# Where the output projection's units stand among the cached blocks of a hybrid decoder step

## The chip, the cores and the metric

The kernel runs on one core of a Trainium2 chip, in one launch. The metric is the device time of the launch in microseconds (us). TensorE (PE in the profile) multiplies, VectorE (DVE), ScalarE (ACT) and GpSimd (POOL) work elementwise and reduce, SyncE (SP) issues most transfers. Each engine runs its own instructions in the order in which the program holds them, and waits on semaphores for the others.

## The reference, cut to what matters

One decoder layer is computed for a prompt of 1024 rows (`x_prompt`, 1024 wide) and for 8 sequences of 8 new rows (`x_sample`, 64 rows), in 32 bits:

```python
n = rmsnorm(h, lw['g_mix']);  u = n @ lw['w_in']          # split for the two groups
o_gla = ...   # group A: gated linear attention, 512 wide
o_mla = attend(q_m, k_m, v_m)                             # group B: latent attention, 512 wide
h = h + jnp.concatenate([o_gla, o_mla], axis=-1) @ lw['w_o']   # the output projection
y, conv_new = conv_ffn(rmsnorm(h, lw['g_ffn']), conv_prev, lw)
h = h + y
h = h + (p @ lw['ple_w_proj']) * jax.nn.sigmoid(rmsnorm(h, lw['g_ple']) @ lw['ple_w_gate'])
```

For the prompt `attend` is a causal attention over its own rows. For each of the 8 sequences it goes over 8192 cached positions in 64 pages of 128, found by a page table: of each page, keys and values are projected from a latent of 128 numbers, the keys normed, and scores, softmax and values summed. The same `w_o` serves the prompt's rows and the sample rows.

## The kernel before, in words

**Numbers in two halves.** A 32-bit operand is split into a high and a low part (`split`, L116 on ACT for the high part, L117 on DVE or POOL for the low one), and a product is three matmuls, high by high, high by low, low by high (`mm3`, L137 to L139).

**Two streams.** The generator `cache_stream` (L646) goes over 64 blocks of 8 pages each, numbered n = 0 to 63, eight to a sequence. A block takes two steps: in the first its pages 4 to 7 are turned by transposes (`pre`: tile ctp L518, and for the rope part crp L496 and csr L506) and pages 0 to 3 go through `main` (L526); in the second the next block's pages 0 to 3 are turned and this block's pages 4 to 7 go through `main`. The first block of a sequence has the new rows as a ninth page. In `main` a page has two products `ks` of three matmuls each (320 and 256 columns), of which ACT takes the squares (tile csq, L542) and the scores (sn, L544); after every second page DVE reduces the squares (css, L547). One and two blocks later come `stage_b` (the norms, and the maximum tile ml, L568, once per block), `stage_c1` (tile mt, exponents, tile phl) and `stage_pv` (tile cpv, L612). `ks` has three PSUM banks; ctp, crp, csr, mt and cpv share two (`pm`); the dense work has three (`pd`).

The generator `dense` (from L1332) does everything else up to the feed-forward: projections, linear attention, prompt attention (`prompt_attention`, tiles S, t, o), and last `wo_prompt` (L1482). A loop written by hand (L1540 to L1554) interleaves the two: each `yield` of the dense stream gives its cost, each cache step adds 4.4 times the stage's `PACE` to the time at which the next is due, and the stream that is behind gets its turn. When the dense stream is used up, the remaining cache steps follow alone.

**The planner.** What the loop gives out is program order. A list scheduler then arranges each engine's instructions by readiness in its own model of time, with program order as the priority. `tc.keep_in_program_order(m)` pins an instruction: it can't stand ahead of the instruction given out just before it on its engine.

**The output projection before.** The mixed outputs lie transposed in DRAM (`doT`, 1024 x 1024), in eight chunks of 128 rows; chunk c is multiplied with rows c of `w_o`. `wo_chunk` (L1377) loads one chunk whole: its rows (tiles oraw, then sh and sl, 1024 columns) and its weights (tiles stg, then wdh and wdl). `down` (L1389) does one pair of chunks for all eight row tiles t and both column halves f: a unit is six matmuls of 512 columns into ps_dn and one addition to `h` on DVE (L1400). `wo_prompt` gives out pairs 0 to 2 so, 48 units in 24 yields of cost 2.6, unpinned, with two calls of `down_sample` (L1405, tile ps_ds) for the sample rows; then it loads chunks 6 and 7. The last pair's 16 units (`last_pair`, L1517, pinned) are kept as filling: `fill(k)` gives out k of them at the waits of the last block (L583 to L691: 4, 1, 3, 2 and 2), and the last four follow. Each finished row tile is normed (`normed`, L1510) for the feed-forward.

After the blocks, the attention of the sample rows is projected (po_mla, L684), `w_o`'s chunks 4 and 5 are loaded again for them, and the rows are turned for the feed-forward, whose matmuls begin near 1401 us.

Of the kernel before, what the change touches and what calls it, by code (L numbers as in the profile page):

```python
# [18 lines left out]
P = 128  # L19
D = 1024  # L20
# [25 lines left out]
def step_kernel(ctx: ExitStack, tc: tile.TileContext, A):  # L46
# [68 lines left out]
    def split(hi, lo, src, lo_eng=None):  # L115
        act.copy(hi, src)  # L116
        (lo_eng or dve).tensor_tensor(lo, src, hi.bitcast(F32), ALU.subtract)  # L117
# [18 lines left out]
    def mm3(ps, ah, al, bh, bl, first=True, last=True):  # L136
        pe.matmul(ps, ah, bh, start=first, stop=False)  # L137
        pe.matmul(ps, ah, bl, start=False, stop=False)  # L138
        pe.matmul(ps, al, bh, start=False, stop=last)  # L139
# [386 lines left out]
    def main(o, g0, cT):  # L526
        buf = o.b % 2
        if g0 == 0:
            o.sn = cp.tile([P, 9, 64], F32, tag="sn", name="sn", bufs=3)
            o.ss = cp.tile([P, 9, 8], F32, tag="css", name="css", bufs=2)  # L530
        gn = min(4, o.nt - g0)
        cTh, cTl = cT
        for i in range(gn):
            if i % 2 == 0:
                sq2 = cp.tile([P, 2, 512], F32, tag="csq", name="csq", bufs=2)
            sq = sq2[:, i % 2]
            for f in range(2):
                ks = psK.tile([P, 512], F32, tag="k", name="ks")
                w = 256 if f else 320
                mh, ml = (m[:, f * 320:f * 320 + w] for m in mv[buf])  # L540
                mm3(ks[:, :w], cTh[:, i, :], cTl[:, i, :], mh, ml)
                act.activation(sq[:, f * 256:f * 256 + 256], ks[:, 0:256], AF.Square)  # L542
                if f == 0:
                    act.copy(o.sn[:, g0 + i, :], ks[:, 256:320])  # L544
            if i % 2 or i == gn - 1:
                n = i % 2 + 1
                dve.tensor_reduce(o.ss[:, g0 + i + 1 - n:g0 + i + 1, :].rearrange("p i h -> p (i h)"),  # L547
                                  sq2[:, :n].rearrange("p i (h n) -> p (i h) n", n=64), AX.X, ALU.add)

    def stage_b(o):  # L550

# [24 lines left out]
    def stage_c1(o):  # L576

        nt = o.nt
        sb = o.sn[:, :nt, :]
        mt = pm([P, 512], "mt")  # L580
        final = (o.b, o.bi) == (NB - 1, 7)
        if final:
            fill(4)  # L583
        pe.transpose(mt[:, 0:P], o.ml.rearrange("p a c -> p (a c)"), ident)
        m = cp.tile([P, 1], F32, tag="bm", name="bm", bufs=4)
        mo = state.get(o.b)
        if mo is None:
# [10 lines left out]
        pool.tensor_tensor(phl[:, :nt, 64:128], sb, phl[:, :nt, 0:64].bitcast(F32), ALU.subtract)  # L598
# [733 lines left out]
    def dense():  # L1332
# [30 lines left out]
    chunks = {}  # L1363

    def stage(shape, dt, name):
        return z["wf"].tile(shape, dt, tag="stage", name=name, bufs=3)
# [4 lines left out]
    def fold_tile(shape, dt, name):  # L1371
        return z["wf"].tile(shape, dt, tag="fd", name=name, bufs=1)

    def wdown(rows):
        return tuple(w[:, 0] for w in wload(z["wf"], rows, 1, D, "wd", 2, 3, stg))

    def wo_chunk(c):  # L1377
        sh = z["wf"].tile([P, T], F32R, tag="sh", name="sh", bufs=3)
        sl = z["wf"].tile([P, T], F32R, tag="sl", name="sl", bufs=3)
        for c0 in range(0, T, 512):  # L1380
            raw = stage([P, 512], F32, "oraw")
            sp.dma_start(raw, doT[c * P:(c + 1) * P, c0:c0 + 512])
            split(sh[:, c0:c0 + 512], sl[:, c0:c0 + 512], raw)
        chunks[c] = (sh, sl, oTg[:, c] if c < 4 else None) + wdown(A["w_o"][0][c * P:(c + 1) * P, :])

    def hrows(t):
        return z["h"][:, t, :] if t < NT else z["hs"]

    def down(grp, bank, order, after=None):  # L1389

        h = z["h"]
        for t in order:
            tt = slice(t * P, (t + 1) * P)
            for f in range(2):
                cs = slice(f * 512, (f + 1) * 512)
                ps = bank([P, 512], "ps_dn")
                for i, c in enumerate(grp):
                    sh, sl, _, wdh, wd = chunks[c]
                    mm3(ps, sh[:, tt], sl[:, tt], wdh[:, cs], wd[:, cs], i == 0, i == len(grp) - 1)
                dve.tensor_tensor(h[:, t, cs], h[:, t, cs], ps, ALU.add)  # L1400
            if after is not None:
                after(t)
            yield 2.6

    def down_sample(parts, bank):  # L1405

        for f in range(2):
            cs = slice(f * 512, (f + 1) * 512)
            ps = bank([P, 512], "ps_ds")
            for i, (ss_, wdh, wd) in enumerate(parts):  # L1410
                pe.matmul(ps, ss_, wdh[:, cs], start=i == 0, stop=False)
                pe.matmul(ps, ss_, wd[:, cs], start=False, stop=i == len(parts) - 1)
            fold_sample(ps, f)

    def fold_sample(ps, f):
        hs = z["hs"][:, f * 512:(f + 1) * 512]
# [62 lines left out]

    room = {}  # L1480

    def wo_prompt():  # L1482

        opened("fx")
        room["hp"] = opened("hp")
        residual(z["hp"])
        room["wf"] = opened("wf", 2)
        room["fb"] = opened("fb")
        for g in range(3):
            grp = (2 * g, 2 * g + 1)  # L1490
            for c in grp:
                wo_chunk(c)
            if g == 0:
                for t in range(NT):
                    sp.dma_start(hrows(t), A["x_prompt"][0, t * P:(t + 1) * P, :])
                sp.dma_start(z["hs"], A["x_sample"].rearrange("b t d -> (b t) d"))
            yield from down(grp, pd, range(NT))
            if g < 2:
                down_sample([chunks[c][2:] for c in grp], pd)
# [14 lines left out]
        sp.dma_start(dh[t], x)  # L1514
        xnorm(t, x, pool if VIAP >> t & 1 else dve)

    def last_pair():  # L1517

        for t in order:
            tt = slice(t * P, (t + 1) * P)  # L1520
            for f in range(2):
                cs = slice(f * 512, (f + 1) * 512)
                ps = pd([P, 512], "ps_dn")
                for i, c in enumerate((6, 7)):
                    sh, sl, _, wdh, wd = chunks[c]
                    m = pe.matmul(ps, sh[:, tt], wdh[:, cs], start=i == 0, stop=False)
                    if i == 0:
                        tc.keep_in_program_order(m)
                    pe.matmul(ps, sh[:, tt], wd[:, cs], start=False, stop=False)
                    pe.matmul(ps, sl[:, tt], wdh[:, cs], start=False, stop=i == 1)  # L1530
                dve.tensor_tensor(z["h"][:, t, cs], z["h"][:, t, cs], ps, ALU.add)
                if f:
                    normed(t)
                yield
# [35 lines left out]
    def both(shape, name):  # L1570
# [1 line left out]
        return (pd, pm, pd, pm, pd, p2)[turn[0]](shape, name)  # L1572

    tw = opened("tw", side="right")
    w45 = [(z["oTm"][:, c - 4],) + tuple(w[:, 0] for w in wload(z["tw"], A["w_o"][0][c * P:(c + 1) * P, :], 1, D, "w45", 2, 3, stg))
           for c in (4, 5)]
    down_sample(w45 + [(z["oTm"][:, c - 4],) + chunks[c][3:] for c in (6, 7)], pm)
    tw.close()


# [458 lines left out]
```

## Time and profile before

| what | value |
|---|---|
| time, median of 3 runs (lowest, highest) | 2287.79 us (2287.11, 2289.05) |
| the profiled execution's own time | 2291.95 us |
| its span, first to last instruction | 2290.0 us |
| granted TensorE clock, mean | 0.981 |
| share of the span busy: PE, DVE, ACT, POOL | 95%, 72%, 58%, 54% |

The span is what the views of the trace cover; the time of an execution holds 2 us more. Times in the views are microseconds from the start of the span. A view of windows gives, for each stretch, its length, each engine's busy time with the number of instructions, the granted clock, and the share and rate of the transfers. A view of groups gives for each line, engine and tile the count, the busy time and the mean in ns of one instruction, and behind the bar the idle time ahead of them with what ended it. In a timeline a row has its start, its duration, engine, line and tiles (out<-in), and in brackets a wait ahead of it. Records of matmuls overlap, since they are pipelined; a few are missing.

### The profile page before, as it was taken

The numbers are of one execution on the slowest core, as the hardware profiler recorded it, in microseconds if no ns is written. First come the engines' busy times: TensorE is split into PE (matmuls) and PEld (weight loads), VectorE is DVE, ScalarE is ACT, GpSimd is POOL, SyncE is SP. The second block draws the span as 40 slices with busy tenths as digits, with TensorE's granted clock in tenths as the row PEclk, the third lists the DMA queues.
The fourth block names the chain that finished last, engine by engine and source line by source line (L and its number), as shares of the span: only waits on it lengthen the run. The fifth ranks groups of instructions, "written<-read, shape, count | busy, mean of one in ns | idle before, by whom it ended". The sixth has DMA issues, their size and how long they took to land.

```text
span 2290.0 us, 38701 instructions
## 1 busy us (share of the span) xinstructions
PE 2173.6 (95%) x13591; PEld 1963.1 (86%) x13591; DVE 1657.5 (72%) x2608; ACT 1335.5 (58%) x3711; POOL 1238.1 (54%) x1332
## 2 busy tenths in 40 slices
PE   7999999999999999999998876999999999999999
PEld 6889878878888888887787766999999997888899
DVE  4675776477788888887787667878888875777642
ACT  5576766777788888887657755333333334222531
POOL 5575668567777777776334547665666640010200
PEclk9899999999999999999999997999999999999999
DMA  5343344413232222214222112322223223433131
GB/s 179 103 141 102 88 128 146 130 49 95 81 94 75 62 65 68 58 45 148 89 87 63 45 74 83 102 97 93 93 92 98 88 84 120 122 118 119 49 116 40
DMA packets 193459, 213.42 MB, mean 93 GB/s; under 512 B 41198, under 2 KB 145107, under 8 KB 193267
## 3 DMA queue, kind: packets, MB, share of 16 engines
q1 hardware_dynamic: 180835, 168.47, 24.1%
q0 software_dynamic: 12432, 42.48, 6.1%
q8 instruction: 109, 1.79, 0.3%
q14 instruction: 83, 0.68, 0.1%
HBM read 168.34 MB, written 42.52 MB: 92 GB/s over the span
## 4 chain that ended last, share of the span: by engine, by line
PE 75%; DVE 8%; ACT 7%; POOL 4%; DMA 3%; issue 2%; SPq 0%; POOLq 0%; DVEq 0%; ACTq 0%
PE ps_gu L139 6%; PE ps_gu L138 6%; PE ps_gu L137 6%; PE ks L137 4%; PE ps_dn L137 4%; PE ps_dn L138 4%; PE ps_dn L139 4%; PE ks L139 4%; PE ks L138 4%; PE cpv L612 2%; DVE css L547 2%; ACT csq L542 2%; PE ctp L518 2%; PE ps_pj L137 2%; PE ps_lt L276 2%
## 5 line engine op out<-in xcount | busy, mean ns | idle before, releaser
L542 ACT ACTIVATE csq<-ks 128x256 f32<-128x256 f32 x1040 | 391.3, 400 | 104.4 <-PE ks L139 96.9
L547 DVE TENSOR_REDUCE css<-csq 128x16 f32<-128x1024 f32 (+1 forms) x264 | 315.7, 1196 | 68.7 <-ACT csq L542 65.5
L116 ACT CAST wh<-st 128x512 fp32r<-128x512 f32 x176 | 108.2, 621 | 160.0 <-PE ps_gu L138 154.0
L574 POOL TENSOR_TENSOR chl<-craw,chl 128x1024 fp32r<-128x1024 f32 x64 | 141.8, 2216 | 93.4 <-ACT chl L573 88.4
L137 PE MATMUL ks<-mv1h,cTh 128*128 128x320 f32 (+1 forms) x520 | 169.9, 330 | 14.7 <-ACT cTh L116 6.8
L137 PE MATMUL ks<-mv0h,cTh 128*128 128x320 f32 (+1 forms) x520 | 169.6, 329 | 9.5 <-ACT csq L542 4.1
L138 PE MATMUL ks<-mv1l,cTh 128*128 128x320 f32 (+1 forms) x520 | 153.0, 297 | 0.0
L138 PE MATMUL ks<-mv0l,cTh 128*128 128x320 f32 (+1 forms) x520 | 152.0, 295 | 0.0
L139 PE MATMUL ks<-mv0h,cTl 128*128 128x320 f32 (+1 forms) x520 | 145.1, 298 | 2.8 <-DVE cTl L117 2.7
L139 PE MATMUL ks<-mv1h,cTl 128*128 128x320 f32 (+1 forms) x520 | 143.8, 300 | 3.6 <-DVE cTl L117 3.5
L1842 DVE TENSOR_TENSOR h<-h,ps_dn 128x512 f32<-128x512 f32 x160 | 107.4, 685 | 47.1 <-PE ps_dn L139 41.6
L137 PE MATMUL ps_dn<-w,s 128*128 128x512 f32 x352 | 136.6, 393 | 2.4 <-ACT w L116 2.4
L117 DVE TENSOR_TENSOR wl<-st,wh 128x512 fp32r<-128x512 f32 x132 | 114.6, 871 | 33.2 <-ACT wh L116 33.2
L138 PE MATMUL ps_dn<-w,s 128*128 128x512 f32 x352 | 137.8, 392 | 0.0
L139 PE MATMUL ps_dn<-w,s 128*128 128x512 f32 x352 | 137.1, 391 | 0.0
L137 PEld LDWEIGHTS ks<-mv1h,cTh 128*128 128x128 f32 x520 | 99.3, 191 | 30.8 <-ACT sn L544 11.9
L117 DVE TENSOR_TENSOR cTl<-ctp,cTh 128x512 fp32r<-128x512 f32 (+1 forms) x136 | 90.1, 662 | 46.8 <-ACT cTh L116 45.7
L1853 POOL TENSOR_TENSOR h<-h,raw 128x512 f32<-128x512 f32 x16 | 20.7, 1296 | 188.1 <-DMA raw<-dh 188.1
L137 PEld LDWEIGHTS ks<-mv0h,cTh 128*128 128x128 f32 x520 | 98.4, 189 | 24.1 <-ACT sn L544 6.8
L544 ACT COPY sn<-ks 128x64 f32<-128x64 f32 x520 | 116.8, 225 | 0.0
L1286 POOL TENSOR_TENSOR pl<-p,ph 128x512 fp32r<-128x512 f32 (+1 forms) x96 | 97.4, 1020 | 33.7 <-DVE ph L1285 20.3
L598 POOL TENSOR_TENSOR phl<-sn,phl 128x512 fp32r<-128x512 f32 (+1 forms) x64 | 84.8, 1326 | 52.4 <-ACT phl L597 52.0
(669 smaller groups left out, 7920.6 us busy)
## 6 DMA issues: line engine op xcount, KB each, us to landing
stage<-w_in SPq DMA_DIRECT2D x48, 256.0 KB
st<-ffn_w_gate SPq DMA_DIRECT2D x44, 256.0 KB
st<-ffn_w_up SPq DMA_DIRECT2D x44, 256.0 KB
wr<-ffn_w_down SPq DMA_DIRECT2D x44, 256.0 KB
raw<-ds SPq DMA_DIRECT2D x44, 256.0 KB
raw<-ffn_w_down SPq DMA_DIRECT2D x44, 256.0 KB
ds<-cv SPq DMA_DIRECT2D x21, 512.0 KB
stg<-w_o SPq DMA_DIRECT2D x20, 256.0 KB
```

What stands on the lines that cost most here:

```text
L116: act.copy(hi, src)
L117: (lo_eng or dve).tensor_tensor(lo, src, hi.bitcast(F32), ALU.subtract)
L137: pe.matmul(ps, ah, bh, start=first, stop=False)
L138: pe.matmul(ps, ah, bl, start=False, stop=False)
L139: pe.matmul(ps, al, bh, start=False, stop=last)
L542: act.activation(sq[:, f * 256:f * 256 + 256], ks[:, 0:256], AF.Square)
L544: act.copy(o.sn[:, g0 + i, :], ks[:, 256:320])
L547: dve.tensor_reduce(o.ss[:, g0 + i + 1 - n:g0 + i + 1, :].rearrange("p i h -> p (i h)"), sq2[:, :n].rearrange("p i (h n) -> p (i h) n", n= ...
L574: pool.tensor_tensor(ch[:, c0:c1, 128:256], src, ch[:, c0:c1, 0:128].bitcast(F32), ALU.subtract)
L598: pool.tensor_tensor(phl[:, :nt, 64:128], sb, phl[:, :nt, 0:64].bitcast(F32), ALU.subtract)
L1286: pool.tensor_tensor(pl[:, c0:], p[:, c0:], ph[:, c0:].bitcast(F32), ALU.subtract)
L1842: dve.tensor_tensor(h[:, t, cs], h[:, t, cs], ps, ALU.add)
```

## The change

- `wo_prompt` is no longer part of the dense stream. Only the allocation of its memory (`wo_room`) stands at the end of `dense`, which has no yield; the stream so ends with the prompt attention.
- The projection is a generator of its own, `wo_units`, that gives out one unit at each call of `next`. Its first call gives out the first loads: rows and weights of chunks 0 and 1, and x.
- `main` calls `place` after every second page. It counts slots, four to a block; past the sixth slot, in three slots of four, it gives out one unit, until 49 calls have been made. A unit's first matmul is pinned, behind the `ks` given out just before.
- What is left of the 49 calls is given out at the last block's `stage_c1`, ahead of the four units that were given out there already. The last pair's 16 units are the same generator's last part, and are filled in as before.
- Rows and weights are loaded and split by halves of 512 columns: `wo_rows(c, n)` and `wo_cols(c, f)`, each with two buffers for each half, one for either chunk of a pair. A pair goes through four quarters of four units, (row half, column half), and the next pair's halves are loaded after the second, third and fourth quarter.
- The loop's condition `ncache < 129` goes.

The diff, cut to its core:

```diff
@@ main
                 dve.tensor_reduce(o.ss[:, g0 + i + 1 - n:g0 + i + 1, :].rearrange("p i h -> p (i h)"),
                                   sq2[:, :n].rearrange("p i (h n) -> p (i h) n", n=64), AX.X, ALU.add)
+                if "fill" in z and n == 2:
+                    place()
+
+    def place():
+
+        z["slot"] += 1
+        if z["slot"] > 6 and z["slot"] % 4 and z["units"] < 49:
+            fill(1)
@@ stage_c1
         if final:
+            fill(49 - z["units"])
             fill(4)
@@ dense
-        yield from wo_prompt()
+        wo_room()
@@
+    def wo_rows(c, n):
+
+        hl = [z["wf"].tile([P, 512], F32R, tag=f"s{n}{k}", name=f"s{k}", bufs=2) for k in "hl"]
+        raw = stage([P, 512], F32, "oraw")
+        sp.dma_start(raw, doT[c * P:(c + 1) * P, n * 512:n * 512 + 512])
+        split(*hl, raw)
+        wos[c, n] = hl
+
+    def wo_cols(c, f):
+
+        hl = [z["wf"].tile([P, 512], F32R, tag=f"wd{f}{k}", name=f"wd{k}", bufs=2) for k in "hl"]
+        raw = stage([P, 512], F32, "wraw")
+        sp.dma_start(raw, A["w_o"][0][c * P:(c + 1) * P, f * 512:f * 512 + 512])
+        split(*hl, raw)
+        wow[c, f] = hl
+    def wo_unit(grp, t, f):
+
+        n, tt, cs = t // 4, slice(t % 4 * P, t % 4 * P + P), slice(f * 512, f * 512 + 512)
+        ps = pd([P, 512], "ps_dn")
+        for i, c in enumerate(grp):
+            (sh, sl), (wh, wl) = wos[c, n], wow[c, f]
+            m = pe.matmul(ps, sh[:, tt], wh, start=i == 0, stop=False)
+            if i == 0:
+                tc.keep_in_program_order(m)
+            pe.matmul(ps, sh[:, tt], wl, start=False, stop=False)
+            pe.matmul(ps, sl[:, tt], wh, start=False, stop=i == len(grp) - 1)
+        h = z["h"][:, t, cs]
+        dve.tensor_tensor(h, h, ps, ALU.add)
+    def wo_units():
+
         for g in range(3):
             grp = (2 * g, 2 * g + 1)
+            f0 = g % 2
+            quarters = ((0, f0), (0, 1 - f0), (1, 1 - f0), (1, f0))
+            for q, (n, f) in enumerate(quarters):
+                if g == 0 and q == 0:
+                    for ld, x in ((wo_rows, 0), (wo_cols, 0)):
+                        for c in grp:
+                            ld(c, x)
+                    for t in range(NT):
+                        sp.dma_start(hrows(t), A["x_prompt"][0, t * P:(t + 1) * P, :])
+                        if t == 3:
+                            for ld, x in ((wo_cols, 1), (wo_rows, 1)):
+                                for c in grp:
+                                    ld(c, x)
+                    sp.dma_start(z["hs"], A["x_sample"].rearrange("b t d -> (b t) d"))
+                    yield
+                for t in range(4 * n, 4 * n + 4):
+                    wo_unit(grp, t, f)
+                    if q == 2 and t == 4 and g < 2:
+                        for e in range(2):
+                            down_sample([(oTg[:, c], wow[c, e]) for c in grp], pd, e)
+                    yield
+                nx = (grp[0] + 2, grp[1] + 2)
+                for c in nx:
+                    if q == 1:
+                        wo_rows(c, 0)
+                    elif q == 2:
+                        wo_cols(c, 1 - f0)
+                    elif q == 3:
+                        wo_cols(c, f0)
+                        wo_rows(c, 1)
             if g == 0:
                 conv_state()
                 gain("g_ffn")
-        wo_chunk(6)
-        wo_chunk(7)
+        for t in order:
+            for f in range(2):
+                wo_unit((6, 7), t, f)
+                if f:
+                    normed(t)
+                yield
@@ the loop
     def fill(n):
         for _ in range(n):
-            next(z["fill"], None)
+            z["units"] += next(z["fill"], done) is None
...
-        if live_c and (not live_d or due <= tdense and ncache < 129):
+        if live_c and (not live_d or due <= tdense):
...
-                z["fill"] = last_pair()
+                z["fill"], z["units"], z["slot"] = wo_units(), 0, 0
+                fill(1)
```

More of the change, by code (lines that the diff above doesn't have):

```diff
@@ L1359, in dense @@
         z["part"] = 7
-        yield from wo_prompt()
-    chunks = {}
+        wo_room()
+    chunks, wos, wow = {}, {}, {}
     def stage(shape, dt, name):
@@ L1372, in fold_tile @@
         return z["wf"].tile(shape, dt, tag="fd", name=name, bufs=1)
[L1374 to L1384, printed above, removed]
+    def wo_rows(c, n):
[4 more added lines that the diff above has]
+        wos[c, n] = hl
@@ L1386, in hrows @@
+    def wo_cols(c, f):
[4 more added lines that the diff above has]
+        wow[c, f] = hl
     def hrows(t):
         return z["h"][:, t, :] if t < NT else z["hs"]
[L1389 to L1413, printed above, removed]
+    def wo_unit(grp, t, f):
[10 more added lines that the diff above has]
+        dve.tensor_tensor(h, h, ps, ALU.add)
@@ L1415, in fold_sample, with down_sample @@
+    def down_sample(parts, bank, f):
+        ps = bank([P, 512], "ps_ds")
+        for i, (ss_, (wh, wl)) in enumerate(parts):
+            pe.matmul(ps, ss_, wh, start=i == 0, stop=False)
+            pe.matmul(ps, ss_, wl, start=False, stop=i == len(parts) - 1)
+        fold_sample(ps, f)
     def fold_sample(ps, f):
@@ L1480, in step_kernel, with wo_room @@
     room = {}
-    def wo_prompt():
+    def wo_room():
         opened("fx")
@@ L1488, in wo_prompt @@
         room["fb"] = opened("fb")
+    def wo_units():
         for g in range(3):
             grp = (2 * g, 2 * g + 1)
[L1491 to L1499, printed above, removed]
+            f0 = g % 2
[28 more added lines that the diff above has]
+                        wo_rows(c, 1)
             if g == 0:
@@ L1515, in normed @@
         xnorm(t, x, pool if VIAP >> t & 1 else dve)
[L1517 to L1534, printed above, removed]
     def fill(n):
         for _ in range(n):
-            next(z["fill"], None)
+            z["units"] += next(z["fill"], done) is None
     dn = dense()
@@ L1553, in step_kernel @@
             if not live_d:
-                z["fill"] = last_pair()
+                z["fill"], z["units"], z["slot"] = wo_units(), 0, 0
+                fill(1)
+                print("cache steps at the end of dense", ncache)
     convT, prv, cout = (z[k] for k in ("convT", "prv", "cout"))
@@ L1574, in step_kernel @@
     tw = opened("tw", side="right")
-    w45 = [(z["oTm"][:, c - 4],) + tuple(w[:, 0] for w in wload(z["tw"], A["w_o"][0][c * P:(c + 1) * P, :], 1, D, "w45", 2, 3, stg))
-           for c in (4, 5)]
-    down_sample(w45 + [(z["oTm"][:, c - 4],) + chunks[c][3:] for c in (6, 7)], pm)
+    w45 = [wload(z["tw"], A["w_o"][0][c * P:(c + 1) * P, :], 1, D, "w45", 2, 3, stg) for c in (4, 5)]
+    for f in range(2):
+        down_sample([(z["oTm"][:, c], [w[:, 0, f * 512:f * 512 + 512] for w in w45[c]]) for c in (0, 1)] +
+                    [(z["oTm"][:, c - 4], wow[c, f]) for c in (6, 7)], pm, f)
     tw.close()
```

## The prediction

> **What bounds the kernel now.** First the head of the page, for the whole span.
>
> ```profile
> span 2290.0 us, 38701 instructions
> PE 2173.6 (95%) x13591; PEld 1963.1 (86%) x13591; DVE 1657.5 (72%) x2608; ACT 1335.5 (58%) x3711; POOL 1238.1 (54%) x1332
> ```
>
> PE looks full, so a change that adds and removes no instruction seems to have 5% to play for at most. That average hides three stages. The next view is the windows: the attention over the prompt beside the cached blocks, the output projection beside them, and the blocks alone. Columns: window, length, then busy time with counts. Below it the same windows for L568 alone, which runs once per block, so that its count is a number of blocks.
>
> ```profile
> core 0: us, PE busy (x) PEld busy (x) DVE busy (x) ACT busy (x) POOL busy (x), PEclk, DMA share, GB/s
> 853.80:1045.30 191.50, 187.78 (x1303) 165.09 (x1301) 162.14 (x262) 166.61 (x500) 143.76 (x151) 1.00 0.20 55
> 1099.60:1197.70 98.10, 95.00 (x538) 81.38 (x537) 78.91 (x120) 57.70 (x171) 34.54 (x29) 1.00 0.27 84
> 1224.90:1320.60 95.70, 80.83 (x526) 70.91 (x526) 66.42 (x106) 73.43 (x246) 53.52 (x46) 0.96 0.15 45
> ...
> 853.80:1045.30 191.50, 12.00 (x11) 1.00 0.20 55
> 1099.60:1197.70 98.10, 4.28 (x4) 1.00 0.27 84
> 1224.90:1320.60 95.70, 7.51 (x8) 0.96 0.15 45
> ```
>
> Each window begins and ends at such a start (the third holds both its ends, so 7 blocks). A block takes 191.5/11 = **17.4 us** beside the attention, 98.1/4 = **24.5 us** beside the projection, and 95.7/7 = **13.7 us** alone. Alone no engine is full: PE 84%, ACT 77%, DVE 69%. PE is emptier still than its row says, as the timeline of PE shows.
>
> ```profile
> 1253.05 0.31 PE L138 MATMUL ks<-mv1l,cTh 128*128 128x320 f32 x1
> 1253.20 0.31 PE L139 MATMUL ks<-mv1h,cTl 128*128 128x320 f32 x1
> 1253.35 0.28 PE L137 MATMUL ks<-mv1h,cTh 128*128 128x256 f32 x1
> 1253.46 0.28 PE L138 MATMUL ks<-mv1l,cTh 128*128 128x256 f32 x1
> ...
> 1254.14 1.25 PE L612 MATMUL cpv<-chl,phl 128*128 128x258 f32 x9
> 1255.23 0.27 PE L518 MATMUL ctp<-ident,craw 128*128 128x128 f32 x1
> ...
> 1364.18 0.39 PE L1526 MATMUL ps_dn<-wdh,sh 128*128 128x512 f32 x1
> 1365.55 0.39 PE L1526 MATMUL ps_dn<-wdh,sh 128*128 128x512 f32 x1
> ```
>
> Records last 0.28 to 0.39 us but overlap; what a matmul costs is the distance to the next start: 0.15 us for 320 columns, 0.115 for 256, 1.09/9 = 0.12 for cpv. The last two rows are one unit of six matmuls of 512 columns apart: **1.37 us** a unit. A block has 48 ks matmuls, 24 x 0.15 + 24 x 0.115 = 6.3 us, and 27 others (8 cpv, 8 ctp, 2 crp, 6 csr, 3 mt; 526/7 = 75 in all) at 0.12, 3.2 us: **9.5 us** of PE in 13.7, so 4.2 us are free, not the 2.1 that the busy column leaves ((95.7 - 80.83)/7). The Trainium skill's page Perfetto Trace Analysis (Identifying the Most-Contended Engine) says that matmul busy time is no good measure and LDWEIGHTS busy time a better one; here that is 74% of the window against 84%, and would leave 3.5 us a block. The rows of waits say what fills the time:
>
> ```profile
> PE ks L137 <- ACT cTh L116: 4.4, 11, 0.7
> PE ks L137 <- ACT sn L544: 4.0, 10, 0.6
> PE ks L139 <- DVE cTl L117: 2.8, 4, 0.7
> ```
>
> They are waits of at most 0.7 us on the two splits and on the PSUM bank that ACT reads: a chain across engines, into whose gaps other PE work fits.
>
> **The change part by part.** It moves work and adds none: 48 units of 6 matmuls, 32 loads of 256 KB with their splits, 9 loads of x, 16 last units. Before, the units run in a narrow stretch:
>
> ```profile
> 1074.81 0.39 PE L137 MATMUL ps_dn<-wdh,sh 128*128 128x512 f32 x1
> ...
> L1400 DVE TENSOR_TENSOR h<-h,ps_dn x48: 671/686/690, 1096.1 to 1216.4; 128x512 f32<-128x512 f32 x48
> ...
> 1099.60:1197.70 98.10, 55.98 (x211) 37.08 (x210) 23.41 (x35) 0.00 (x0) 1.00 0.27 84
> 1099.60:1197.70 98.10, 4.46 (x16) 2.73 (x16) 2.67 (x4) 2.34 (x4) 1.00 0.27 84
> ```
>
> The last two rows are the tiles ps_dn and ps_ds (sample rows) in the second window: 211/6 = 35 units in 4 blocks, 8.8 a block. After, dense work ends with the attention; counted from the loop (each yield's cost against 4.4 x PACE) 95 cache steps are then out, so that block 47 is next. Slots are four a block; those over 6 and not divisible by 4 from block 47 to 63 are 46. Two more units go to the final block's c1, ahead of its old 4.
>
> *Where the units go.* Block 48 reduces at 1066.3 and block 49 at 1083.5, block 63 at 1332.3:
>
> ```profile
> 1066.34 1.17 DVE L568 TENSOR_REDUCE ml<-sn 128x64 f32<-128x576 f32 x1
> 1083.48 1.09 DVE L568 TENSOR_REDUCE ml<-sn 128x64 f32<-128x512 f32 x1
> L568 DVE TENSOR_REDUCE ml<-sn x64: 1031/1075/1195, 114.0 to 1332.3; 128x64 f32<-128x512 f32 x56, 128x64 f32<-128x576 f32 x8
> ```
>
> The attention ends as before and the loads still follow its end, so block 48 stays and block 49 ends at some 1081 (15 us, between 13.7 alone and the 17.1 here). Then 14 blocks carry the 46 units, and the sample rows of two groups (16 matmuls, 2.7 units' worth): 3.5 units, 4.8 us of PE a block. Their length from three sides:
> - PE: 9.5 + 4.8 = 14.3 us. In the second window PE did 227 matmuls of 512 columns (211 + 16) at 0.228 and 311 of the others at 0.125: 91 of 98.1 us, 93%. 14.3/0.93 = 15.4.
> - DVE: 66.4/7 = 9.5 us, plus 3.3 additions of 0.686 and 1.6 for splits and sample rows (rows below), 13.4; at the 85% that it reaches beside the attention (162.14/191.5) 15.8.
> - The chord between stages: beside the attention 3.7 us more a block, for these tiles' PE time (S, o and t):
>
> ```profile
> 853.80:1045.30 191.50, 38.00 (x171) 23.57 (x138) 0.00 (x0) 23.21 (x47) 0.00 (x0) 1.00 0.20 55
> 853.80:1045.30 191.50, 37.21 (x136) 19.89 (x136) 4.74 (x7) 4.18 (x7) 1.00 0.20 55
> 853.80:1045.30 191.50, 31.08 (x158) 16.76 (x127) 39.32 (x68) 11.79 (x20) 1.00 0.20 55
> ```
>
> 106.3/11 = 9.7 us of busy a block, against 55.98/35 = 1.6 for a unit: like 6.1 units. 3.5 of them cost 3.7 x 3.5/6.1 = 2.1: 15.8.
>
> I take **15.7** (bounds: 14.3, PE without a gap; 17.4, as beside the attention). 14 x 15.7, less 2 for the last block, which has no successor (1320.6 to 1332.3 is 11.7), is 218: block 63 reduces at 1299 in place of 1332, **-33 us**. Where the cover is gone (no gap in PE at all) a unit costs 1.37 us, and the move gains nothing.
>
> *The splits by halves.* Same number, other places:
>
> ```profile
> L117 DVE TENSOR_TENSOR wdl<-stg,wdh 128x512 fp32r<-128x512 f32 x8 | 7.7, 967 | 1.6 <-ACT wdh L116 1.6
> L117 DVE TENSOR_TENSOR sl<-oraw,sh 128x512 fp32r<-128x512 f32 x10 | 6.9, 707 | 0.4 <-ACT sh L116 0.4
> L116 ACT CAST wdh<-stg 128x512 fp32r<-128x512 f32 x8 | 5.0, 632 | 1.7 <-DMA stg<-w_o 1.7
> ```
>
> 20 of them fall into the 14 blocks: 20 x 0.84/14 = 1.2 us of DVE each (in the sum above, with 0.4 for the sample rows: the 2.67 of the ps_ds row and as much again for the sum's other half), 0.9 of ACT, whose 10.5 (73.43/7) becomes 11.4 of 15.7. SP issues the same 41 DMAs, the first pair's rows and weights ahead of x; behind a load that waits for a stage buffer only loads of this part and block 56's new rows are queued on SP. POOL's queue, with the blocks' own loads, is not touched.
>
> *The added wait.* Rows and weights of the next pair take buffers that the current pair's quarter gives up. Eight or four units, 36 or 18 us, lie between load and use, except at the end: the last pair begins with the half that the 48th unit still uses. Four splits then follow that unit, 0.63 + 4 x 0.97 = 4.5 us, with the units of the final block queued behind on PE. That block's chain partly covers it:
>
> ```profile
> 1324.77 0.28 PE L139 MATMUL ks<-mv1h,cTl 128*128 128x256 f32 x1
> ...
> 1345.99 1.24 PE L612 MATMUL cpv<-chl,phl 128*128 128x258 f32 x8 [0.40 <-POOL phl L598]
> ```
>
> 21 us from the last ks to the last cpv, released by POOL, with 8 last units in between (11 us); two more units (2.7) and 4.5 of splits make 18. So between 0 and 7 us; I take **+4**, as the additions and norms of the last rows move too.
>
> **Sum:** -33 + 4 = -29. The profiled execution took 2291.95 us for a span of 2290.0; it becomes 2263, and the median, 4 us below it (2287.79), **2259 us**. The clock is 0.96 in the third window against 1.00 in the others; full, it would give up to 0.4 us a block, 5 us in all, not in the sum.
>
> **The rivals.** *A: the chain grows with the units.* A unit stands between a block's matmuls, and ctp, crp, mt and cpv share two PSUM banks, so that its 1.37 us may lengthen the chain rather than fill a gap. For: the attention's 17.4 with DVE at 85%. Against: ACT had 15.1 us a block there, here 11.4. At 17.4 to 17.9 a block 63 reduces at 1323 to 1330: -9 to -2, with +4 to +7 at the end 2283 to 2293.
>
> *B: pinned units that wait, slower.* A pinned unit can't be overtaken backwards: where its split is late, all ks behind it on PE stand, and the whole chain. Before, a change of groups did this once:
>
> ```profile
> 1130.00:1140.00 10.00, 7.86 (x48) 6.25 (x46) 8.45 (x11) 8.45 (x25) 4.79 (x4) 1.00 0.51 160
> ...
> 1140.04 2.63 DMA stg<-w_o
> 1142.69 0.63 ACT wdh L116
> ```
>
> There are 9 later half-loads. Exposed in full, each costs 2.63 + 0.63 + 0.97 = 4.2 us: 38 in all, 2297; it decides from 29/9 = 3.2 us each. Against: 18 us and more of cover. The Trainium skill's page TensorE: Matmul & The Clock Gate (Part 2, on LDWEIGHTS) says that matmuls stay in program order, only weight loads being pulled ahead, which speaks against pinning; no row of this trace shows one overtaking another.
>
> *C: the change doesn't spread.* A pin only keeps a unit from going earlier. If the units slip and stand in a crowd late in the stretch, as at 8.8 a block before, their time is as before: 2288.
>
> **How the numbers follow.** Forecast, blocks of 14.3 to 17.4: -53 to -9 in the stretch, +2 to +6 at the end, so 2237 to 2285, chance 0.70. A 0.10, B 0.15, C 0.05. No change is within 0.2% (4.6 us, 2283 to 2292), about what a measurement of this kernel can tell. Faster: the forecast without its last 2 us, 0.69. Same: that end, A and C, 0.16. Slower: B, 0.15. The range, 2240 to 2290, leaves out B, the forecast's far end (0.03) and a little of A (0.02).
>
> **What would show it.** Right: L568 starts 15 to 16.5 us apart from block 49 to 62, and block 63's near 1300; PE's 84% alone rising over 93%; three ps_dn groups a block, with its additions spread to the end. A shows as 17 us and more with DVE or ACT naming most of PE's waits; B as waits of PE on s or wd splits, over 2 us each; C as additions crowded. The tail is right if the last cpv follows the last ks by 21 to 28 us.

## The result: a little slower, and the profile after

| | before | after |
|---|---|---|
| time, median (lowest, highest), 6 runs each | 2288.26 us (2287.11, 2292.58) | 2299.07 us (2296.36, 2301.83) |
| ratio, 95% interval | | 1.0045 [1.0032, 1.0058] |
| the profiled execution's own time, span | 2291.95, 2290.0 us | 2298.32, 2296.1 us |
| maximum of block 52, block 62, block 63 | 1153.1, 1320.6, 1332.3 | 1137.2, 1326.1, 1339.2 |
| from block 63's maximum to the feed-forward's first matmul | 68.7 us | 69.1 us |

Slower by 10.8 us, against 29 us faster in the forecast. (The two profiled executions differ by 6.4 only: the one of before lies 3.7 us above its median, the one of after 0.7 below.) In them block 63 comes 6.9 us later, and the way from there to the feed-forward takes 0.4 us longer, so the whole change lies in the blocks. First the head of the page of after, then its windows for blocks 52 to 62, with L576 (L568 before, once a block) below, both edges counted, so 10 blocks.

```profile
span 2296.1 us, 38695 instructions
PE 2179.3 (95%) x13591; PEld 1966.0 (86%) x13591; DVE 1658.8 (72%) x2608; ACT 1339.8 (58%) x3711; POOL 1240.0 (54%) x1332
```

```profile
core 0: us, PE busy (x) PEld busy (x) DVE busy (x) ACT busy (x) POOL busy (x), PEclk, DMA share, GB/s
1137.20:1326.10 188.90, 165.87 (x961) 141.93 (x961) 124.83 (x200) 121.93 (x381) 78.38 (x67) 0.95 0.18 55
...
1137.20:1326.10 188.90, 10.56 (x11) 0.95 0.18 55
...
1137.20:1326.10 188.90, 51.51 (x180) 35.27 (x180) 20.41 (x31) 0.00 (x0) 0.95 0.18 55
```

The shares of the whole span tell nothing: all are as before. The windows do. The last row is ps_dn: 180/6 = 30 units in 10 blocks, three each, so the units are spread just as the change says. But a block takes 188.9/10 = **18.9 us**, not 15.7, and PE's share rises only from 84% to 88%. Alone a block took 13.7, so three units and the sample rows cost 5.2 us, where their matmuls take 4.3 (180 of units and 8 of sample rows in 10 blocks, at 0.228). They filled nothing and made the blocks a little longer still.

The same can be read from distances between starts. If each matmul of the window is given its back-to-back distance (0.228 us for 512 columns, 0.15, 0.115 and so on), what is left of the window is time in which PE stands still, or is slowed by its clock: by this estimate 32.1 us in before's 7 blocks alone, **4.6 a block**; 52.5 us in these 10, **5.25 a block**. The gap that the forecast meant to fill is still there, whole. The clock is a small part: a mean of 0.96 loses 3.8 of before's 95.7 us, 0.5 a block, and 0.95 loses 9.4 of after's 188.9, 0.9 a block. The waits of PE in this window say where it stands still (us in total, times, longest):

```profile
PE ks L139 <- DVE cTl L117: 8.9, 7, 2.3
PE ks L137 <- ACT cTh L116: 7.8, 18, 2.0
PE ks L137 <- ACT sn L544: 3.7, 10, 0.4
```

The two splits still lead, and their longest waits have grown from 0.7 to 2.3 and 2.0 us. The timeline shows one such place, on PE, ACT and DVE.

```profile
1284.94 0.28 PE L139 MATMUL ks<-mv1h,cTl 128*128 128x256 f32 x1
1285.06 0.39 PE L1408 MATMUL ps_dn<-wdh,sh 128*128 128x512 f32 x1
...
1286.19 0.39 PE L1412 MATMUL ps_dn<-wdh,sl 128*128 128x512 f32 x1
1286.42 0.60 PE L518 MATMUL ctp<-ident,craw 128*128 128x128 f32 x4
1286.95 0.43 PE L602 MATMUL mt<-ident,bm 64*128 64x64 f32 x2
1287.70 0.41 PE L137 MATMUL ks<-mv1h,cTh 128*128 128x320 f32 x1 [0.31 <-ACT cTh L116]
...
1288.48 0.31 PE L138 MATMUL ks<-mv1l,cTh 128*128 128x320 f32 x1
1289.92 0.68 PE L139 MATMUL ks<-mv1h,cTl 128*128 128x320 f32 x3 [1.14 <-DVE cTl L117]
```

```profile
1284.00 0.59 ACT L506 COPY sr<-csr 128x512 f32<-128x512 f32 x1
...
1287.06 0.59 ACT L116 CAST cTh<-ctp 128x512 fp32r<-128x512 f32 x1 [1.20 <-PE ctp L518]
```

```profile
1287.03 0.68 DVE L1414 TENSOR_TENSOR h<-h,ps_dn 128x512 f32<-128x512 f32 x1
1287.62 1.05 DVE L576 TENSOR_REDUCE ml<-sn 128x64 f32<-128x512 f32 x1
1288.59 0.68 DVE L603 TENSOR_TENSOR sn<-sn,mt 128x512 f32<-128x512 f32 x1
1289.18 0.68 DVE L117 TENSOR_TENSOR cTl<-ctp,cTh 128x512 fp32r<-128x512 f32 x1
```

Read it from the end. The products `ks` with cTl wait 1.14 us for cTl; cTl for cTh and for its turn on DVE; cTh for the four transposes ctp, on which ACT waited 1.20 us. And ctp, at 1286.42, stands behind a whole unit (1285.06 to 1286.42). So the unit isn't in the gap. It stands ahead of the instruction that starts the chain, and the gap opens behind that instruction. The unit's own addition then stands on DVE ahead of the maximum and of cTl.

Why is ctp so late? It shares two PSUM banks with csr, crp, mt and cpv, which the program gives out in turn. crp and csr come once a block, when the next block's pages 0 to 3 are turned (and not with pages 4 to 7, as the description of the kernel before has it). The ctp of pages 4 to 7 is the second tile behind csr (mt lies between) and so takes its bank: it can go only when ACT has copied csr out (L506). Then this ctp, cTh, cTl and the next group's `ks` follow one from another, in PE's order. On the chip the copy shown above had ended at 1284.59, before the unit began; that ctp stands behind the unit is the order that the planner chose in its own model of time. Of the three units in a block, the one behind the first pair of pages 0 to 3 stands between csr's products or close by them, and the one behind the second pair ahead of this ctp. Both lie on this loop. The block's other ctp (at 1296.18) is followed after 0.35 us by `ks` that use an earlier split, and the wait for its own cTh is 0.21 us.

**Theory "series":** a unit ahead of csr or ctp lengthens the loop by its whole length, while the waits behind ctp stay; behind ctp it would be free. **Rivals:** "additions" (DVE's 0.68 us a unit ahead of cTl is the cost, not PE's place), the halves (the finer loads and splits, or quarters), and the pin itself.

### The profile page after: what moved, and what is told of

Its sections match the earlier page's. It is cut to its first block, busy times and chain, and to the rows that moved or that the text cites. A ratio compares the mean times of both kernels' runs of the same rounds, so it can differ in the third digit from the quotient of the medians.

```text
span 2296.1 us, 38695 instructions
## 1 busy us (share of the span) xinstructions
PE 2179.3 (95%) x13591; PEld 1966.0 (86%) x13591; DVE 1658.8 (72%) x2608; ACT 1339.8 (58%) x3711; POOL 1240.0 (54%) x1332
## 4 chain that ended last, share of the span: by engine, by line
PE 76%; DVE 9%; ACT 7%; DMA 3%; POOL 2%; issue 2%; SPq 0%; POOLq 0%; DVEq 0%; ACTq 0%
PE ps_gu L139 6%; PE ps_gu L138 6%; PE ps_gu L137 6%; PE ks L137 5%; PE ks L138 4%; PE ks L139 4%; PE ps_dn L137 4%; PE ps_dn L139 4%; PE ps_dn L138 4%; PE cpv L621 2%; DVE css L547 2%; ACT csq L542 2%; PE ctp L518 2%; PE ps_pj L137 2%; PE ps_lt L276 1%
## 5 line engine op out<-in xcount | busy, mean ns | idle before, releaser
L137 PE MATMUL ks<-mv0h,cTh 128*128 128x320 f32 (+1 forms) x520 | 170.7, 332 | 10.8 <-ACT sn L544 4.3
```

## The experiments

The times below are medians of up to ten runs; ratios are against before on the same chip (2288.78 us in the first group, 2288.21 and 2289.57 in the others), with their 95% intervals. Block 63 stands for the time of its maximum: 1339.2 in after, 1332.3 in before.

### The parts of the change

**e4: the halves alone.** The new loads, quarters and order, but the 48 units given out in the dense stream as before, unpinned.

```diff
 # main: no place();  stage_c1: no fill(49 - z["units"])
+        z["fill"], z["units"], z["slot"] = wo_units(), 0, 0
+        fill(1)
+        for u in range(48):
+            fill(1)
+            if u % 2:
+                yield 2.6
-            if i == 0:
+            if i == 0 and c > 5:
                 tc.keep_in_program_order(m)
```

> Loads by halves, quarters and the new order of units alone: the 48 units are given out in the dense stream at a cost of 2.6 for two, unpinned, as in the kernel before. Theory 'place': the halves cost nothing and gain little: 2284 to 2292 us. Rival 'halves': 2296 to 2302 us.

Measured: 2287.25 us, 0.9994 [0.9984, 1.0004]. The halves cost nothing and bring nothing; the loss comes with giving the units out among the blocks.

**e1: the pin taken off the 48 units.**

```diff
-            if i == 0:
+            if i == 0 and c > 5:
                 tc.keep_in_program_order(m)
```

> The 48 units are not pinned (the last pair's 16 still are); slots, loads and halves stay. Theory 'place': the change lost because each pinned unit stands directly behind a pair's products and ahead of the next transposes (ctp) or of csr, so it lengthens the block's chain by its whole 1.37 us and leaves the gaps behind ctp empty. Unpinned, the planner pulls the units forward into a crowd soon after the attention, as in the kernel before: 2283 to 2292 us, blocks of 20 us and more first and of 13 to 14 us after. Rival 'halves': the loads by halves cost the 11 us, wherever the units stand: 2296 to 2302 us.

Measured: 2287.75 us, 0.9993 [0.9983, 1.0003]. The windows of ps_dn:

```profile
1066.00:1228.00 162.00, 82.96 (x312) 57.67 (x312) 35.02 (x52) 0.00 (x0) 0.97 0.37 125
...
1228.00:1320.00 92.00, 0.00 (x0) 0.00 (x0) 0.00 (x0) 0.00 (x0) 0.96 0.14 42
```

52 of the 64 units stand before 1228 us, none from there to 1320. Unpinned the planner draws them together again, as before, and the time is that of before. So the pin does spread them, and by that it costs 11 us.

**e3: nearly no additions.** The additions of the 48 units take one column of 512; this leaves most of the sum into `h` out.

```diff
-        dve.tensor_tensor(h, h, ps, ALU.add)
+        if c > 5:
+            dve.tensor_tensor(h, h, ps, ALU.add)
+        else:
+            dve.tensor_tensor(h[:, 0:1], h[:, 0:1], ps[:, 0:1], ALU.add)
```

> As the changed kernel, but the addition behind each of the 48 units takes one column of 512 (the rest of the sum is left out), so that DVE is freed of some 0.6 us a unit while every order stays nearly as it is. Theory 'place': PE's order is the cause, DVE only follows: 2293 to 2299 us, blocks of 18 us and more. Rival 'additions': 0.69 us of DVE ahead of ml, the subtraction and cTl is what holds PE: 48 x 0.6 is up to 29 us, time 2270 to 2288 us, and PE's waits for cTl fall from 8.9 us to under 4 in the same stretch.

Measured: 2288.26 us, 1.0000 [0.9990, 1.0010]; block 63 at 1328.9, a block 17.9 us. Its waits, blocks 52 to 62:

```profile
PE ks L137 <- ACT cTh L116: 10.4, 18, 1.9
PE ks L137 <- ACT sn L544: 4.2, 11, 0.4
PE ks L139 <- DVE cTl L117: 2.0, 3, 1.1
```

The window of these blocks:

```profile
1136.60:1315.80 179.20, 158.71 (x965) 135.56 (x964) 110.36 (x201) 122.11 (x382) 77.82 (x67) 0.99 0.19 58
```

48 x 0.6 = 29 us less of DVE bring 10.8 us: the wait for cTl goes from 8.9 to 2.0 us, that for cTh stays, even grows. This missed both ranges: it is faster than theory "place" allowed, it lies 0.3 us above the rival's range, and the rival's sign, waits for cTl under 4 us, came. So the additions are a part of the cost, at most 1.0 us a block. They are not all of it: blocks without them still take 17.9 us, 4.2 more than alone, about what the units' matmuls take. How much of the 1.0 is theirs isn't shown, since the granted clock differs too: 0.99 here, 0.95 in after, which by the lengths of the windows is up to 7.6 of the 9.7 us between them (an estimate: 9.4 us lost there, 1.8 here).

### What a unit costs where it stands

**e10 and e11: one unit of each block made narrow.** 128 of 512 columns, so that part of the product is left out, with the addition kept on other data: in e10 the unit behind the second pair (ahead of ctp), in e11 that behind the first (ahead of csr).

```diff
 # place():  z["at"] = z["slot"] % 4 around fill(1), then 0
+        w = 128 if z.get("at", 0) == 2 else 512      # e11: == 1
-            m = pe.matmul(ps, sh[:, tt], wh, start=i == 0, stop=False)
+            m = pe.matmul(ps[:, :w], sh[:, tt], wh[:, :w], start=i == 0, stop=False)
...
-        dve.tensor_tensor(h, h, ps, ALU.add)
+        dve.tensor_tensor(h, h, ps if w == 512 else z["h"][:, (t + 4) % 8, cs], ALU.add)
```

> As the changed kernel, but the unit behind the second pair of pages 0 to 3 takes 128 of its 512 columns (three quarters of that part of the product are left out; its addition stays as long, on other data): 6 x 0.17 = 1.0 us less of PE in 15 blocks. Theory 'series': it stands in the loop in full, so 15 us and no less: 2281 to 2286 us. Rival 'it is half hidden': 2290 to 2295 us. Rival 'it costs only by its addition': 2297 to 2301 us.

> The same for the unit behind the first pair, three quarters of its columns left out, its addition as long. Theory 'series' (this unit stands ahead of csr): 2281 to 2287 us. Rival 'only a unit directly ahead of ctp costs in full, this one stands in a gap': 2294 to 2301 us.

Measured: e10 2287.1 us, 0.9991 [0.9980, 1.0003]; e11 2285.39 us, 0.9979 [0.9966, 0.9993]. One narrow unit of e10, with the instruction behind it:

```profile
1292.79 0.22 PE L1411 MATMUL ps_dn<-wdh,sh 128*128 128x128 f32 x1
...
1293.19 0.28 PE L1414 MATMUL ps_dn<-wdl,sh 128*128 128x128 f32 x1
1293.30 0.27 PE L1415 MATMUL ps_dn<-wdh,sl 128*128 128x128 f32 x1
1293.51 0.43 PE L604 MATMUL mt<-ident,bm 64*128 64x64 f32 x2
```

The expectations took a quarter of the columns for a quarter of the time. But these matmuls of 128 columns start 0.11 us apart, not 0.057, so a narrow unit takes 0.62 to 0.72 us, and what was taken out is some 0.7 us a unit, 10 to 11 us in 15 blocks and not 15. The time fell by 12.0 and 13.7. So PE time taken out at either place comes back in full: nothing fills it, and nothing hides it. That is also why e10 lies 1.1 us above its range; e11 is inside its own. What fell beyond the price wasn't taken apart; the addition, on other data, no longer waits for its unit, and that may be a part of it.

### The same work behind ctp

**e2: units behind ctp.** The two pinned units of the pairs go to `pre`, behind the splits of ctp, the third to the group's first pair.

```diff
 # pre, behind the split of ctp into cTh and cTl
+        if "fill" in z and g0 < 8 and 48 < o.n:
+            place()
 # main
-                if "fill" in z and n == 2:
-                    place()
+                if "fill" in z and g0 == 0 and i == 1 and 48 < o.n:
+                    fill(1)
 # place()
-        z["slot"] += 1
-        if z["slot"] > 6 and z["slot"] % 4 and z["units"] < 49:
+        if z["units"] < 49:
```

> As the changed kernel, but from block 49 on a unit is pinned directly behind each group's four ctp transposes (two a block) and one behind the first pair of a block, 45 in all; four remain for the last block. Theory 'place': a unit behind ctp fills the wait for the splits cTh and cTl (1 to 1.5 us there in the changed kernel, 52 us idle in 10 blocks): blocks of 16 to 17.5 us in place of 18.9, time 2270 to 2285 us, waits of PE for cTl under 5 us in 10 blocks (12 there by distance of starts). Rival 'additions': DVE's additions, not the place, hold cTl back: 2295 to 2303 us and the waits as they are. Rival 'every unit costs its 1.37 us wherever it stands': 2296 to 2301 us.

Measured: **2273.45 us**, 0.9931 [0.9915, 0.9948]; a block 16.2 us, PE's waits for cTl 0.3 us in blocks 52 to 62, block 63 at 1305.7. All as theory "place" had it. The end gets longer: 77.2 us from block 63's maximum to the feed-forward, against 69.1.

**e8 and e9: one unit of three moved.** e8 moves only the unit that stands ahead of ctp, past the four transposes and into the place behind them; e9 moves only the one of the first pair.

```diff
 # pre, behind the split of ctp
+        if "fill" in z and g0 == 4 and 48 < o.n:
+            fill(1)
 # place()
-        if z["slot"] > 6 and z["slot"] % 4 and z["units"] < 49:
+        if z["slot"] > 6 and z["slot"] % 4 in (1, 3) and z["units"] < 49:   # e9: in (2, 3)
```

> As the changed kernel, but of a block's three units one alone is moved: the one behind the second pair of pages 0 to 3, which the planner puts directly ahead of ctp, is given out and pinned behind that ctp. Theory 'place': moved by four transposes it fills the wait for cTh and cTl behind ctp, 1 to 1.4 us a block over 15 blocks: 2278 to 2285 us. Rival 'all three cost alike, by the additions or in some other way': 2295 to 2301 us.

> As the changed kernel, but the other unit of the first half is moved: the one behind a block's first pair goes behind ctp, the one behind the second pair and the one of the second half stay. In the changed kernel that first unit stands ahead of csr, whose copy frees the PSUM bank that ctp takes. Theory 'series': csr, its copy, ctp, the split and the next products are one loop, so a unit in front of csr costs as much as one in front of ctp, and with it gone ctp is ready before the second unit: 2268 to 2278 us, as with the second unit moved. Rival 'only a unit directly ahead of ctp costs': 2288 to 2300 us. Rival 'a unit behind ctp is what gains, by filling its wait, and the unit ahead of it costs as before': 2280 to 2288 us.

Measured: e8 **2271.32 us**, 0.9924 [0.9908, 0.9941]; a block 15.9, block 63 at 1311.3. e9 2273.22 us, 0.9930 [0.9913, 0.9946]; a block 16.5, block 63 at 1315.2. e8 beats both kernels, by 17 and 28 us, and is the best version found. Its windows, its waits and the same place of a block on PE:

```profile
1136.60:1295.60 159.00, 148.66 (x944) 132.38 (x944) 127.74 (x193) 118.16 (x376) 79.17 (x67) 0.99 0.20 62
```

```profile
PE crp L496 <- DVE pvs L632: 2.7, 4, 1.0
...
PE ks L139 <- DVE cTl L117: 1.1, 1, 1.1
PE ks L137 <- ACT cTh L116: 0.9, 2, 0.7
```

```profile
1249.02 0.28 PE L139 MATMUL ks<-mv1h,cTl 128*128 128x256 f32 x1
1249.13 0.64 PE L518 MATMUL ctp<-ident,craw 128*128 128x128 f32 x4
1249.54 0.49 PE L1410 MATMUL ps_dn<-wdh,sh 128*128 128x512 f32 x1
...
1252.17 0.39 PE L1414 MATMUL ps_dn<-wdh,sl 128*128 128x512 f32 x1
1252.49 0.43 PE L604 MATMUL mt<-ident,bm 64*128 64x64 f32 x2
1252.85 0.41 PE L137 MATMUL ks<-mv1h,cTh 128*128 128x320 f32 x1
...
1253.78 0.57 PE L139 MATMUL ks<-mv1h,cTl 128*128 128x320 f32 x3
```

ctp now follows the last ks at once, two units stand behind it, and when they are done both splits lie ready: no brackets on the `ks` rows. PE's idle time by distances is 25.7 us in these 10 blocks, half of after's 52.5; the waits for cTh and cTl together fall from 16.7 to 2.0. In e9 too two units end up behind ctp, the second one by the planner's choice. e8 came out 7 us below its expectation; in the rows above the unit that wasn't moved ends up behind ctp as well.

**e6: ctp in another bank.** After as it is, pins included, but ctp of the stretch takes one of the dense work's three banks.

```diff
-        tp = pm([P, 4, P], "ctp")
+        tp = (pd if "fill" in z else pm)([P, 4, P], "ctp")
```

> As the changed kernel, units where it has them, but once the dense work is done the transposes ctp take a PSUM bank of the dense work's three in place of one of the two that cpv, crp, csr and mt share. Theory 'bank': ctp stands at the end of a group, with the wait for its own splits behind it, because its bank comes free only after csr and its copy; with a bank of its own it goes out half a block ahead, the waits for cTh and cTl vanish and the same pinned units cost less than their 1.37 us: blocks of 15 to 16.5 us, 2255 to 2275 us. Rival 'place alone': a pinned unit behind a pair lengthens the chain wherever ctp stands: blocks of 18 us and more, 2292 to 2302 us.

Measured: 2275.02 us, 0.9945 [0.9928, 0.9961]; a block 15.9, block 63 at 1312.5. Window and waits:

```profile
1143.10:1302.50 159.40, 152.91 (x963) 135.65 (x963) 126.42 (x197) 120.21 (x387) 77.72 (x67) 0.99 0.22 65
```

```profile
PE ks L137 <- ACT sn L544: 1.7, 3, 0.8
...
PE ks L139 <- DVE cTl L117: 0.8, 1, 0.8
```

The units stay pinned where the change gives them out, yet the wait for cTh is gone from the list, and 24 us with it. The timeline of PE shows why:

```profile
1255.53 0.60 PE L518 MATMUL ctp<-ident,craw 128*128 128x128 f32 x4
1255.89 0.39 PE L137 MATMUL ks<-mv1h,cTh 128*128 128x320 f32 x1
...
1258.13 0.60 PE L518 MATMUL ctp<-ident,craw 128*128 128x128 f32 x4
```

`ks` starts 0.36 us behind ctp, sooner than a cTh of 0.59 us could be ready, so it uses an earlier split: with csr's copy out of its way the planner has ctp run a group ahead, and two sets of transposes are out within 2.6 us. The shared bank is what tied the loop. The time is at the edge of its range, with blocks inside theirs. It isn't better than e8 though the blocks are as short, since they begin later: block 47 came at 1066.9 instead of 1045.0 and block 52 at 1143.1 (1137.2 in after). No ctp stands between 1035 and 1049.6, while the attention's last tiles run, whose banks it now shares; that it queues for them is likely, but no wait of PE shows it. The Trainium skill's page Perfetto Trace Analysis (Optimization Strategy) says that a gap which repeats over a stretch can mean too few PSUM buffers for the next tile; this run agrees with it, by 24 us.

### Two that missed

**e5: e2 from one block earlier**, to start the units sooner and relieve the end. **e7: e5 with e6's bank.**

```diff
-        if "fill" in z and g0 < 8 and 48 < o.n:                 # e2
+        if "fill" in z and g0 < 8 and 47 < o.n:                 # e5 and e7
-                if "fill" in z and g0 == 0 and i == 1 and 48 < o.n:
+                if "fill" in z and g0 == 0 and i == 1 and 47 < o.n:
-        tp = pm([P, 4, P], "ctp")                               # e7 only
+        tp = (pd if "fill" in z else pm)([P, 4, P], "ctp")
```

> As the kernel with units behind ctp, but begun one block earlier, so that all 48 units are out before the last block and the last pair's halves are loaded and split before its units are given out. Theory: in that kernel the last block is 8 us longer than in the changed one since its late units and the four late splits stand in it (from the last ks to the last cpv 29.6 us against 21.8); begun earlier, that comes back: 2264 to 2270 us, and 20 to 24 us from the last ks to the last cpv. Rival 'the end is set by the block's own chain on POOL and DVE': 2271 to 2276 us.

> Units behind ctp from block 48 on, and ctp in a bank of the dense work's three. Theory 'bank': most of the gain is the bank's, the place adds little: 2252 to 2266 us. Theory 'place': the bank adds nothing to the kernel with units behind ctp from block 48: 2264 to 2272 us.

Measured: e5 2277.59 us, 0.9957 [0.9943, 0.9971]; e7 2289.08 us, 0.9999 [0.9989, 1.0008].

e5's end shortened as expected (from the last `ks` to the last cpv 20.4 us, against 29.6 in e2), but its last block took 24.6 us, so that block 63 came at 1322.6. There cpv waits for the exponents:

```profile
1315.86 1.23 PE L622 MATMUL cpv<-chl,phl 128*128 128x258 f32 x8 [2.41 <-POOL phl L608]
```

That wait is a tenth of the block. Why the planner ordered the last two blocks so wasn't settled. In e7 block 48 alone took 27.8 us, to 1098.8. Its waits from 1060 to 1110, and one of the rest:

```profile
PE ps_dn L1409 <- ACT wdh L116: 3.7, 1, 3.7
...
PE ctp L518 <- DVE h L1415: 0.7, 2, 0.5
...
PE ctp L518 <- DMA craw<-cache_ckv,idx: 4.8, 4, 2.8
```

The first unit waits 3.7 us for its weights' split, and ctp waits for additions to empty the banks that it now shares with the units. These sum to well under the lost time. Part of the rest is what e6 lost at the same place: block 47 came at 1071.0, against 1043.8 in e5, which differs by the bank alone. By block 63 7.5 us of these 27.2 are left, and the end takes 74.5 us against 64.9; why isn't settled. What is shown is that the two remedies don't add up.

## Why the prediction was wrong

**The step that failed is the length of the 14 blocks**, 15.7 us in the forecast, 18.9 measured. Worked back: block 49 at 1083.6 (forecast 1081) is 2.6 us; 13 blocks to block 62 took 242.5 us instead of 204.1, 38.4 us; the last took 13.1 instead of 13.7. Together 40 us, block 63 at 1339 instead of 1299. The other terms nearly cancel: the end takes 3.6 us less than forecast and what follows it 0.9 less, while the forecast put the median 4.2 us below the profiled execution and that of after lies 0.7 above its own.

**What was wrong in the step.** All three estimates took PE and DVE as capacity to be filled: work plus units, over a share that the engine reaches elsewhere. They agreed (15.4, 15.8, 15.8) because they shared that assumption, so their agreement was no support. The 93% and the chord came from stages where the planner itself put unpinned matmuls into the gaps. A pinned unit stands no earlier than it was given out, and that was by csr and ahead of ctp, while the gaps lie behind ctp. The forecast's own condition, that without cover a unit costs 1.37 us and the move gains nothing, is what happened: 13.7 and the matmuls' 4.3 are 18.0 of the 18.9; for the other 0.9 the lower clock (0.4 a block more is lost than before) and the additions were found, not told apart. The free time itself was no error: with the place (e8) or the bank (e6) changed, a block takes 15.9 us with nearly the same units in it (172/6 = 28.7 and 186/6 = 31 in 10 blocks).

**What was right.** The stage is bound by a chain, with the split waits at its head; 4.2 us free a block (4.6 by distances); three units a block, so rival C is out; halves and their splits at nothing (e4); the attention's end and block 48 as before (1066.0 against 1066.3).

**The end**, +4 in the forecast, was +0.4 in after, with one wait of 1.1 us of a unit on a late half. In e2, which leaves more units to the last block, it was +8; e8 stands at 69.6 us, near after. How many are left over isn't all of it: with none, e5 has 64.9 us and e7 74.5.

**The rivals.** A was the mechanism: it named the two banks shared by ctp, crp, mt and cpv, and its sign came, over 17 us a block with DVE and ACT named in PE's waits. Its price was too low, since it stopped at the attention's 17.9 us a block, where units cost at most what the attention's tiles cost. Full price for three units and sample rows (13.7 + 4.3 = 18.0) and a little for the lengthened cTl wait was the bound to take. B gave the nearest time, 2297, by luck: its mechanism isn't there, no wait of PE on s or wd is listed from 1070 to 1326. The Trainium skill's rule that matmuls stay in program order (TensorE: Matmul & The Clock Gate, Part 2), set beside B, belonged beside A: in the rows above ctp came 1.36 us after the unit's first matmul, with all six of them ahead of it.

**Against e8.** 2271 is still 12 us above the forecast, and so is its block 63, at 1311.3: 3.5 us are block 49, 5 the next three (52.1 us from 1084.5 to 1136.6, 17.4 each), 2 the ten of 15.9, and 2 the last, 15.7.

## What to carry to other kernels

Free time of an engine has a place, and filling gains only there. Before work is pinned between a chain's instructions, find which instruction starts the wait, and put the work behind that one, not ahead of it: here giving out one unit behind four transposes instead of ahead of them, where the planner then put a second, was worth 28 us. Ask too what holds that instruction back; here it was a shared PSUM bank, and a bank elsewhere was worth 24 us with no unit moved.

## What the runs showed of the hardware

The granted clock can be halved just when PE begins again. Behind a wait of 3.55 us it is 0.50 in after for 3.4 us, and matmuls of 512 columns are 0.43 us apart, before they are 0.24 apart (the window's row, cpv's row, then the units):

```profile
1336.40:1339.80 3.40, 3.40 (x12) 3.11 (x13) 1.30 (x4) 1.05 (x1) 2.48 (x3) 0.50 0.00 0
...
1336.39 2.09 PE L621 MATMUL cpv<-chl,phl 128*128 128x258 f32 x8 [3.55 <-POOL phl L607]
1338.27 0.63 PE L1408 MATMUL ps_dn<-wdh,sh 128*128 128x512 f32 x1
1338.70 0.63 PE L1411 MATMUL ps_dn<-wdl,sh 128*128 128x512 f32 x1
...
1340.13 0.40 PE L1412 MATMUL ps_dn<-wdh,sl 128*128 128x512 f32 x1
1340.37 0.40 PE L1408 MATMUL ps_dn<-wdh,sh 128*128 128x512 f32 x1
```

Over the blocks the mean clock is 0.95 in after and 0.99 in e6 and e8. That filled gaps keep it up isn't shown: e3, whose PE is as little busy as after's (89% and 88% of these blocks), has 0.99 too.

The cost of a matmul doesn't go on falling with its columns: from start to start 0.228 us for 512, 0.15 for 320, 0.115 for 256, but 0.11 for 128 (e10).
